# A hybrid decoder trunk on one NeuronCore: outputs of the state-space scan by 64-column blocks

## The chip, the core and the metric

The kernel runs on one core of one Trainium2 chip, in float32. The metric is the device time of the whole program in microseconds. The kernel before takes 884.48 us (median of 3 runs, 884.39 to 885.38).

## The reference, cut to what matters

One sequence of 256 steps and 2048 channels goes through an even layer, an odd layer (differential attention) and a final RMSNorm. The even layer projects to 5120 columns; 1024 of them, `xa`, feed 64 groups of 16 channels, each with 64 complex states. Per group, with A = diag(a) from `lam` and `dt`:

```
h[t] = a * h[t-1] + B u[t]          # complex, 64 states
y[t] = Re(C h[t]) + D u[t]
```

`y` goes through gelu and a gate (`w_glu`), and then, beside a second branch, into the output projection. The inputs are scaled so that all parts count.

## The kernel before, in words

All weights stream from HBM by SP's queue into three buffers `wr` (`fetch`, L144). Each chunk is split into a high and a low part: ACT copies it to `wh`, VectorE subtracts to `wl` (`split`, L169, both at high priority), and TensorE multiplies three times (hi x hi, hi x lo, lo x hi). The layer's projections come in the order v, xa, u, gb, ga, then half of the output projection ("eo"), then "glu" (L802), which needs the state-space output, then the rest. Smaller jobs are generators that are run one step at a time between the chunks (`run_side`, L202).

The order of the instructions on TensorE, VectorE, ACT and POOL is laid by the planner of the tile framework, which simulates the program with costs of its own and takes what is ready by priority: program order, and for blocks in `hp()` a head start of 4000 places. A tile waits for the last use of the tile that had its slot (`t8(slot, ...)`; the pool `t4` has three slots). Only SP's order is by hand. In the trace a float32 matmul that is not float32r leaves two records.

The state-space part works on pairs of steps. `ssm_params` (L388) computes `ab` (a, complex), `fc` and `fa` (the input factors for the second and the first step of a pair) on 128 x 32 tiles. `ssm_consts` (L492) fills `bbr[0..1]`, `cA` and `cN` with zeros on POOL and then makes them by products on VectorE (two of m1, two of m2, then one combination each) and masked copies on ACT (`masked`, L487, two per result): `bbr` = B times fc and fa, `cA` = C times a, `cN` = C. Its last step makes `pk0` with 64 matmuls of 32 weight columns and 32 streamed columns (L533 to L535) and adds it on VectorE into `intra` (L536 to L539): the part K0 = Re(C fc B) of an output that comes from inputs of the same pair at the same step, beside D. The part for the other step of the pair comes with the state.

`ssm_set` (L588) is run eight times, for two halves of the groups, two `qh` and two `q`: W = B u by 16 matmuls (L597), a rotation on VectorE (f), a scan (L613), a rotation back (b), and the state `hst` (L620 to L622) for 128 pairs with a zero ahead, 129 columns. Then the outputs: where q = 0, four matmuls with `intra` (L627); then, for each of four column tiles, four matmuls with 32 weight columns and 128 streamed columns (L635): the first step of a pair takes `cA` on the state ahead of the pair (columns 0 to 127), the second takes `cN` on the state of the pair itself (columns 1 to 128). They write the rows q*64 and q*64 + 32 on of `y`. ACT's gelu (`yaf`) ends a pair of sets.

Slots: `xk` (the input by rows) uses b9 and b10 before `cA` and `cN`; `xsq`, the scratch of the first norm's squares, uses b12 before `U2`, which holds the inputs `u` (ACT copies, L712).

Of the kernel before, what the change touches and what calls it, by code (L numbers as in the profile page):

```python
# [10 lines left out]
F32 = mybir.dt.float32  # L11
# [3 lines left out]
ALU = mybir.AluOpType  # L15
# [14 lines left out]
def hybrid_trunk_kernel(ctx: ExitStack, tc: tile.TileContext, xT, xtok, w_in0, w_glu, w_out0,  # L30
                        w_in1, w_out1, pk, bc, lng, wsp, rope, subln, fnorm, out):
    nc = tc.nc
    V, A, PE, G, SP = nc.vector, nc.scalar, nc.tensor, nc.gpsimd, nc.sync
# [6 lines left out]
    sm = ctx.enter_context(tc.tile_pool(name="sm", bufs=1))  # L40
# [7 lines left out]
    def t8(slot, name, shape, dt=F32):  # L48
        return big.tile(shape, dt, name=name, tag=f"b{slot}")
# [13 lines left out]
    def mul(o, a, b):  # L63
        tt(o, a, b, ALU.mult)

    def add(o, a, b):
        tt(o, a, b, ALU.add)

    def sub(o, a, b):
        tt(o, a, b, ALU.subtract)  # L70
# [7 lines left out]
    def stt(o, a, s, b, op0, op1):  # L78
        V.scalar_tensor_tensor(out=o, in0=a, scalar=s, in1=b, op0=op0, op1=op1)
# [272 lines left out]
    def p32(name, w=32, dt=F32, bufs=1):  # L352
        return sm.tile([128, w], dt, name=name, tag=f"p{w}{name}", bufs=bufs)
# [32 lines left out]
    cst = {}  # L386

    def ssm_params():  # L388
        dt_ = p32("dt")
        exact_exp(dt_, log_dt)  # L390
        yield
        mag = p32("mag")
        z = tr32("lrdt")
        mul(z, lam_re, dt_)
        exact_exp(mag, z)
        r2 = p32("r2")
        mul(r2, mag, mag)
        cst["r2"] = r2
        yield
        ph = tr32("ph")  # L400
        mul(ph, lam_im, dt_)
        k = tr32("ph_k")
        ts(k, ph, 1.0 / (2 * math.pi), ALU.mult)
        ts(k, k, MAGIC, ALU.add)
        ts(k, k, MAGIC, ALU.subtract)
        stt(ph, k, -6.28125, ph, ALU.mult, ALU.add)
        stt(ph, k, -1.93500518798828125e-3, ph, ALU.mult, ALU.add)
        stt(ph, k, -(2 * math.pi - 6.28125 - 1.93500518798828125e-3), ph, ALU.mult, ALU.add)
        y = tr32("ph_y")
        ts(y, ph, 0.5, ALU.mult)  # L410
        z = tr32("ph_z")
        mul(z, y, y)
        s = tr32("ph_s")
        f = math.factorial
        ts(s, z, 1.0 / f(13), ALU.mult)
        for c in (-1.0 / f(11), 1.0 / f(9), -1.0 / f(7), 1.0 / f(5), -1.0 / f(3)):
            stt(s, s, c, z, ALU.add, ALU.mult)
        stt(s, s, 1.0, y, ALU.add, ALU.mult)
        c_ = tr32("ph_c")
        ts(c_, z, -1.0 / f(14), ALU.mult)  # L420
        for c in (1.0 / f(12), -1.0 / f(10), 1.0 / f(8), -1.0 / f(6), 1.0 / f(4), -0.5):
            stt(c_, c_, c, z, ALU.add, ALU.mult)
        ts(c_, c_, 1.0, ALU.add)
        ep = p32("ep", 64).rearrange("p (c m) -> p c m", c=2)
        mul(ep[:, 0, :], s, s)
        ts(ep[:, 0, :], ep[:, 0, :], -2.0, ALU.mult, 1.0, ALU.add)
        stt(ep[:, 1, :], s, 2.0, c_, ALU.mult, ALU.mult)
        yield
        ab = p32("ab", 64).rearrange("p (c m) -> p c m", c=2)
        mul(ab, ep, mag.unsqueeze(1).to_broadcast([128, 2, 32]))  # L430
        den = tr32("den")
        t1 = tr32("t1")
        mul(den, lam_re, lam_re)
        mul(t1, lam_im, lam_im)
        add(den, den, t1)
        V.reciprocal(out=den, in_=den)
        nr = tr32("nr")
        ts(nr, ab[:, 0, :], 1.0, ALU.subtract)
        fc = p32("fc", 64).rearrange("p (c m) -> p c m", c=2)
        t2_ = tr32("t2")  # L440
        mul(t1, nr, lam_re)
        mul(t2_, ab[:, 1, :], lam_im)
        add(t1, t1, t2_)
        mul(fc[:, 0, :], t1, den)
        mul(t1, ab[:, 1, :], lam_re)
        mul(t2_, nr, lam_im)
        sub(t1, t1, t2_)
        mul(fc[:, 1, :], t1, den)
        fa = p32("fa", 64).rearrange("p (c m) -> p c m", c=2)
        mul(t1, fc[:, 0, :], ab[:, 0, :])  # L450
        mul(t2_, fc[:, 1, :], ab[:, 1, :])
        sub(fa[:, 0, :], t1, t2_)
        mul(t1, fc[:, 0, :], ab[:, 1, :])
        mul(t2_, fc[:, 1, :], ab[:, 0, :])
        add(fa[:, 1, :], t1, t2_)
        cst.update(ab=ab, fc=fc, fa=fa, ep=ep)
        yield

        pw = []
        prev = ep  # L460
        for j in range(7):
            sq = tr32("pw_sq", (128, 64)).rearrange("p (c m) -> p c m", c=2)
            m = tr32("pw_m")
            mul(sq, prev, prev)
            add(m, sq[:, 0, :], sq[:, 1, :])
            ts(m, m, -1.0, ALU.mult, 2.0, ALU.add)
            e = p32(f"pw{j}", 64).rearrange("p (c m) -> p c m", c=2)
            sub(e[:, 0, :], sq[:, 0, :], sq[:, 1, :])
            stt(e[:, 1, :], prev[:, 0, :], 2.0, prev[:, 1, :], ALU.mult, ALU.mult)
            mul(e, e, m.unsqueeze(1).to_broadcast([128, 2, 32]))  # L470
            pw.append(e)
            prev = e
        cst["pw"] = pw
        yield

    bbr = [None, None]
# [15 lines left out]
    def ssm_consts():  # L492
        for c in range(2):
            bbr[c] = t8(7 + c, f"bbr{c}", [128, 32, 2, 32])
            G.memset(bbr[c], 0.0)
        cA = t8(9, "cA", [128, 2, 32, 32])
        cN = t8(10, "cN", [128, 2, 32, 32])
        G.memset(cA, 0.0)
        G.memset(cN, 0.0)
        cst.update(cA=cA, cN=cN)  # L500
        b_re, b_im, c_re, c_im = (bct[:, i] for i in range(4))
        for gg in range(2):
            r = slice(gg * 64, gg * 64 + 64)
            h = slice(gg * 16, gg * 16 + 16)
            act(cN[r, 0, :, h], c_re[r], AF.Copy)
            act(cN[r, 1, :, h], c_im[r], AF.Copy, scale=-1.0)
        yield
        for key, z_re, z_im, o_re, o_im, sign in (
                ("fc", b_re, b_im, bbr[0][:, :, 1, :], bbr[1][:, :, 1, :], 1.0),
                ("fa", b_re, b_im, bbr[0][:, :, 0, :], bbr[1][:, :, 0, :], 1.0),  # L510
                ("ab", c_re, c_im, cA[:, 0], cA[:, 1], -1.0)):
            s = cst[key]
            m1 = t4(f"m1{key}", [128, 2, 32, 16])
            m2 = t4(f"m2{key}", [128, 2, 32, 16])
            mul(m1[:, 0], z_re, sc16(s[:, 0, :]))
            mul(m1[:, 1], z_im, sc16(s[:, 1, :]))
            mul(m2[:, 0], z_im, sc16(s[:, 0, :]))
            mul(m2[:, 1], z_re, sc16(s[:, 1, :]))
            sub(m1[:, 0], m1[:, 0], m1[:, 1])
            if sign > 0:  # L520
                add(m2[:, 0], m2[:, 0], m2[:, 1])
            else:
                stt(m2[:, 0], m2[:, 0], -1.0, m2[:, 1], ALU.mult, ALU.subtract)
            masked(o_re, m1[:, 0])
            masked(o_im, m2[:, 0])
            yield

        intra = cst["intra"]
        pk0 = side1("pk0", [128, 16, 32])
        for i in range(16):  # L530
            for q in range(2):
                P = i * 2 + q
                o = pk0[q * 64:q * 64 + 32, i, :]  # L533
                PE.matmul(o, bbr[0][:, P, 1, :], cN[:, 0, P, :], start=True, stop=False)
                PE.matmul(o, bbr[1][:, P, 1, :], cN[:, 1, P, :], start=False, stop=True)  # L535
        for q in range(2):  # L536
            r = slice(q * 64, q * 64 + 32)
            o = intra[r, :, q * 64:q * 64 + 32]
            add(o, pk0[r], o)  # L539
        yield  # L540

    def ssm_bT():
# [39 lines left out]
        yield  # L582

    ya = {}
    hst = sm.tile([128, 2, 4, 129], F32, name="hst", tag="hst")
    G.memset(hst[:, :, :, 0:1], 0.0)

    def ssm_set(S):  # L588
        half, q4 = S // 4, S % 4
        qh, q = q4 // 2, q4 % 2  # L590
# [9 lines left out]
        m1 = t4(f"f1{S}", [128, 2, 4, 128])  # L600
        m2 = t4(f"f2{S}", [128, 2, 4, 128])
# [8 lines left out]
        for c in range(2):  # L610
            for ct in range(4):
                P = (half * 2 + qh) * 8 + ct * 2 + q
# [3 lines left out]
        m1 = t4(f"b1{S}", [128, 2, 4, 128])  # L616
        m2 = t4(f"b2{S}", [128, 2, 4, 128])
        mul(m1, g, erb)
        mul(m2, g, eib)
        h = hst  # L620
        sub(h[:, 0, :, 1:129], m1[:, 0], m2[:, 1])
        add(h[:, 1, :, 1:129], m1[:, 1], m2[:, 0])  # L622
        yield
        if q == 0:
            ya["y"] = side1(f"y{S}", [128, 4, 128], 1)
# [3 lines left out]
        y = ya["y"]  # L629
        for ct in range(4):  # L630
            P = (half * 2 + qh) * 8 + ct * 2 + q
            for i, cm in ((0, cst["cA"]), (1, cst["cN"])):
                o = y[q * 64 + i * 32:q * 64 + i * 32 + 32, ct, :]
                for c in range(2):
                    PE.matmul(o, cm[:, c, P, :], h[:, c, ct, i:i + 128], start=False, stop=c == 1,  # L635
                              skip_group_check=True)
        yield
        if q == 1:
            if "f" not in ya:
# [523 lines left out]
```

## Time and profile before

| what | value |
|---|---|
| runs | 884.39, 884.48, 885.38 us |
| the profiled execution | 885.88 us, its span 884.2 us |
| granted TensorE clock in it | 0.998 of full |
| TensorE (PE) busy | 867.1 us, 98% |
| TensorE weight loads (PEld) busy | 748.3 us, 85% |
| VectorE (DVE) busy | 678.4 us, 77% |
| ScalarE (ACT) busy | 457.5 us, 52% |
| GpSimd (POOL) busy | 36.5 us, 4% |

Times are in microseconds from the start of the span unless marked ns. Engines are named as in the table; SP is the engine whose queue issues most transfers. `128*32 128x128` behind a matmul gives its weights (rows and columns) and what is streamed. A row of the timeline has the start, the time to the end of the last of the x instructions merged in it, the engine, the line and the operation with output and inputs, and in brackets the engine's idle time before it with what ended it. Ends of matmuls are modelled and run over the next start. An idle time in brackets of a matmul is what is left after that.

### The profile page before, as it was taken

What the parts mean: (1) busy time and instruction counts of PE and PEld (TensorE: products, weight loads), DVE (VectorE), ACT (ScalarE), POOL (GpSimd) and SP (SyncE); (2) the same over time, 40 slices, a digit from 0 to 9 for tenths busy, and PEclk for the clock granted to TensorE, in tenths of its full rate; (3) what the DMA queues carried; (4) which work ended last, traced back from release to release, by engine and by line L of the source; (5) the groups of instructions that cost most, each with busy time, mean ns of one, the idle gap of its engine ahead of it and who ended that gap; (6) DMA issues with size and microseconds to landing.
All of it is one profiled execution on the core that took longest, in us unless ns stands there. A gap on an engine that the chain in (4) does not pass through costs nothing.

```text
span 884.2 us, 13006 instructions
## 1 busy us (share of the span) xinstructions
PE 867.1 (98%) x5038; PEld 748.3 (85%) x5038; DVE 678.4 (77%) x1248; ACT 457.5 (52%) x637; POOL 36.5 (4%) x54
## 2 busy tenths in 40 slices
PE   9999999999999999999999999999999999999996
PEld 7799978788999789888788888888888888888885
DVE  8999869999988766577876688667867687665773
ACT  6664862455434655565445544455546544564551
POOL 7100000000000100000000000000000000000001
PEclk9999999999999999999999999999999999999999
DMA  8965452235524655555554555445554555555442
GB/s 289 406 236 193 144 191 95 97 103 184 191 99 145 254 178 184 190 191 171 169 203 153 181 191 191 184 153 184 183 192 154 190 182 189 189 194 199 157 178 95
DMA packets 55166, 160.18 MB, mean 181 GB/s; under 512 B 3392, under 2 KB 37440, under 8 KB 41024
## 3 DMA queue, kind: packets, MB, share of 16 engines
q1 hardware_dynamic: 54240, 155.68, 50.1%
q0 software_dynamic: 576, 3.15, 0.9%
q8 instruction: 39, 0.64, 0.3%
q10 hardware_dynamic: 288, 0.52, 0.2%
q14 instruction: 23, 0.19, 0.1%
HBM read 157.24 MB, written 2.10 MB: 180 GB/s over the span
## 4 chain that ended last, share of the span: by engine, by line
PE 87%; DVE 8%; ACT 2%; issue 1%; DMA 1%; DVEq 0%; ACTq 0%
PE k L251 7%; PE q L251 7%; PE v L225 4%; PE v L226 4%; PE v L224 4%; PE k L252 3%; PE q L252 3%; PE g L226 3%; PE g L225 3%; PE g L224 3%; PE od L225 2%; PE od L224 2%; PE od L226 2%; DVE wl L61 2%; PE ga L237 2%; PE ga L240 2%
## 5 line engine op out<-in xcount | busy, mean ns | idle before, releaser
L82 ACT ACTIVATE wh<-wr 128x1024 fp32r<-128x1024 f32 (+1 forms) x276 | 288.7, 1047 | 339.2 <-PE v L226 59.5
L61 DVE TENSOR_TENSOR wl<-wr,wh 128x1024 fp32r<-128x1024 f32 (+1 forms) x276 | 332.3, 1206 | 135.3 <-ACT wh L82 133.8
L251 PE MATMUL k<-h2p,wh 128*128 128x512 f32 x256 | 90.9, 398 | 1.7 <-DVE rm L61 1.7
L251 PE MATMUL q<-h2p,wh 128*128 128x512 f32 x256 | 90.2, 396 | 0.0
L252 PE MATMUL q<-h2p,wl 128*128 128x256 f32 x256 | 71.9, 284 | 0.2 <-DVE wl L61 0.2
L252 PE MATMUL k<-h2p,wl 128*128 128x256 f32 x256 | 72.0, 282 | 0.0
L251 PEld LDWEIGHTS k<-h2p,wh 128*128 128x128 f32 x256 | 48.1, 188 | 13.3 <-DVE rm L61 2.0
L251 PEld LDWEIGHTS q<-h2p,wh 128*128 128x128 f32 x256 | 47.8, 188 | 10.5
L225 PE MATMUL v<-wl,h2p 128*128 128x512 f32 x128 | 50.8, 397 | 0.0
L225 PE MATMUL g<-wl,h2p 128*128 128x512 f32 x128 | 50.3, 393 | 0.0
L226 PE MATMUL g<-wh,h2p 128*128 128x512 f32 x128 | 50.1, 391 | 0.0
L226 PE MATMUL v<-wh,h2p 128*128 128x512 f32 x128 | 50.0, 391 | 0.0
L224 PE MATMUL g<-wh,h2p 128*128 128x512 f32 x128 | 50.0, 390 | 0.0
L224 PE MATMUL v<-wh,h2p 128*128 128x512 f32 x128 | 50.0, 390 | 0.0
L252 PEld LDWEIGHTS q<-h2p,wl 128*128 128x128 f32 x256 | 48.4, 189 | 1.0 <-DVE wl L61 0.6
L252 PEld LDWEIGHTS k<-h2p,wl 128*128 128x128 f32 x256 | 48.4, 189 | 0.1
L225 PE MATMUL od<-wl,oh 128*128 128x512 f32 x96 | 37.6, 392 | 0.0
L224 PE MATMUL od<-wh,oh 128*128 128x512 f32 x96 | 37.5, 391 | 0.0
L226 PE MATMUL od<-wh,ol 128*128 128x512 f32 x96 | 37.3, 390 | 0.0
L237 PE MATMUL ga<-hh,wh 128*128 128x256 f32 x128 | 36.6, 286 | 0.0
L240 PE MATMUL ga<-hh,wl 128*128 128x256 f32 x128 | 36.5, 287 | 0.0
L239 PE MATMUL ga<-hl,wh 128*128 128x256 f32 x128 | 36.5, 285 | 0.0
(330 smaller groups left out, 2041.1 us busy)
## 6 DMA issues: line engine op xcount, KB each, us to landing
wr<-in_w_in_dram SPq DMA_DIRECT2D x68, 1024.0 KB, 4.8
wr<-in_w_in_dram SPq DMA_DIRECT2D x68, 512.0 KB, 5.2
wr<-in_w_out_dram SPq DMA_DIRECT2D x32, 1024.0 KB, 4.8
wr<-in_w_glu_dram SPq DMA_DIRECT2D x4, 1024.0 KB, 4.7
wr<-in_w_in_dram SPq DMA_DIRECT2D x8, 256.0 KB, 4.9
xk<-in_xtok_dram SPq DMA_DIRECT2D x2, 1024.0 KB, 10.8
xr<-in_xtok_dram POOLq DMA_DIRECT2D x2, 1024.0 KB, 7.2
xt<-in_xT_dram SPq DMA_DIRECT2D x8, 128.0 KB, 4.6
```

What stands on the lines that cost most here:

```text
L61: (eng or V).tensor_tensor(out=o, in0=a, in1=b, op=op)
L82: A.activation(out=o, in_=i, func=f, **kw)
L224: PE.matmul(ps[:, t, :], hi[:, s], wh, start=first and a == 0, stop=False)
L225: PE.matmul(ps[:, t, :], hi[:, s], wl, start=False, stop=False)
L226: PE.matmul(ps[:, t, :], lo[:, s], wh, start=False, stop=last and a == len(ktiles) - 1)
L237: PE.matmul(ps[:, c, :], wh[:, s], hi, start=first and a == 0 and c % 2 == 0, stop=False, skip_group_check=True)
L239: PE.matmul(ps[:, c, :], wh[:, s], lo, start=False, stop=False, skip_group_check=True)
L240: PE.matmul(ps[:, c, :], wl[:, s], hi, start=False, stop=fin, skip_group_check=True)
L251: PE.matmul(ps[:, c, :], wh[:, s], hl, start=first and a == 0, stop=False, skip_group_check=True)
L252: PE.matmul(ps[:, c, T:], wl[:, s], hl[:, 0], start=False, stop=a == len(ktiles) - 1 and not first, skip_group_check=True)
```

## The change: the diff

Both steps of a pair now take their state part from the state ahead of the pair: the weights `cc[c]` hold 64 columns per group pair, C a and C a^2 side by side, and the 16 matmuls of a set become 8 with 64 weight columns. What the second step gets from the inputs of its own pair now lies wholly in `intra`: `pk0` is made with `bbr`'s two halves side by side (64 columns), which gives K0 and K1, the part that goes from the first step's input to the second step's output, in the same matmuls, and two more sums put them in place. `a2` = a^2 is computed for it. `cN` stays for `pk0` and moves to slot b12.

```diff
@@ ssm_params
+        a2 = p32("a2", 64).rearrange("p (c m) -> p c m", c=2)
+        mul(t1, ab[:, 0, :], ab[:, 0, :])
+        mul(t2_, ab[:, 1, :], ab[:, 1, :])
+        sub(a2[:, 0, :], t1, t2_)
+        stt(a2[:, 1, :], ab[:, 0, :], 2.0, ab[:, 1, :], ALU.mult, ALU.mult)
-        cst.update(ab=ab, fc=fc, fa=fa, ep=ep)
+        cst.update(ab=ab, a2=a2, fc=fc, fa=fa, ep=ep)
@@ ssm_consts
-        cA = t8(9, "cA", [128, 2, 32, 32])
-        cN = t8(10, "cN", [128, 2, 32, 32])
-        G.memset(cA, 0.0)
-        G.memset(cN, 0.0)
-        cst.update(cA=cA, cN=cN)
+        cc = [t8(9 + c, f"cc{c}", [128, 32, 2, 32]) for c in range(2)]
+        cN = t8(12, "cN", [128, 2, 32, 32])
+        for z in (cc[0], cc[1], cN):
+            G.memset(z, 0.0)
+        cst["cc"] = cc
...
-                ("ab", c_re, c_im, cA[:, 0], cA[:, 1], -1.0)):
+                ("ab", c_re, c_im, cc[0][:, :, 0, :], cc[1][:, :, 0, :], -1.0),
+                ("a2", c_re, c_im, cc[0][:, :, 1, :], cc[1][:, :, 1, :], -1.0)):
...
-                o = pk0[q * 64:q * 64 + 32, i, :]
-                PE.matmul(o, bbr[0][:, P, 1, :], cN[:, 0, P, :], start=True, stop=False)
-                PE.matmul(o, bbr[1][:, P, 1, :], cN[:, 1, P, :], start=False, stop=True)
+                o = pk0[q * 64:q * 64 + 64, i, :]
+                for c in range(2):
+                    PE.matmul(o, bbr[c][:, P].rearrange("p j h -> p (j h)"), cN[:, c, P, :], start=c == 0, stop=c == 1)
         for q in range(2):
-            r = slice(q * 64, q * 64 + 32)
-            o = intra[r, :, q * 64:q * 64 + 32]
+            r = slice(q * 64, q * 64 + 64)
+            o = intra[r, :, q * 64 + 32:q * 64 + 64]
             add(o, pk0[r], o)
+            o = intra[q * 64:q * 64 + 32, :, q * 64:q * 64 + 32]
+            add(o, pk0[q * 64 + 32:q * 64 + 64], o)
@@ ssm_set
-    hst = sm.tile([128, 2, 4, 129], F32, name="hst", tag="hst")
+    hst = sm.tile([128, 2, 4, 128], F32, name="hst", tag="hst")
...
-        sub(h[:, 0, :, 1:129], m1[:, 0], m2[:, 1])
-        add(h[:, 1, :, 1:129], m1[:, 1], m2[:, 0])
+        sub(h[:, 0, :, 1:128], m1[:, 0, :, 0:127], m2[:, 1, :, 0:127])
+        add(h[:, 1, :, 1:128], m1[:, 1, :, 0:127], m2[:, 0, :, 0:127])
...
-            for i, cm in ((0, cst["cA"]), (1, cst["cN"])):
-                o = y[q * 64 + i * 32:q * 64 + i * 32 + 32, ct, :]
-                for c in range(2):
-                    PE.matmul(o, cm[:, c, P, :], h[:, c, ct, i:i + 128], start=False, stop=c == 1,
-                              skip_group_check=True)
+            for c in range(2):
+                PE.matmul(y[q * 64:q * 64 + 64, ct, :], cst["cc"][c][:, P].rearrange("p i h -> p (i h)"),
+                          h[:, c, ct, :], start=False, stop=c == 1, skip_group_check=True)
```

## Rows read from the trace of the kernel before

**Rows 1.** The page, part 4: the chain that ended last, by engine.
```profile
PE 87%; DVE 8%; ACT 2%; issue 1%; DMA 1%; DVEq 0%; ACTq 0%
```

**Rows 2.** Timeline of TensorE, 150 to 154 us: one set's output matmuls.
```profile
150.33 0.30 PE L635 MATMUL y<-hst,cA 128*32 128x128 f32 x1
150.35 0.30 PE L635 MATMUL y<-hst,cN 128*32 128x128 f32 x1
...
152.03 0.27 PE L635 MATMUL y<-hst,cN 128*32 128x128 f32 x1
```

**Rows 3.** Chain that ended last, in order of time: start, us, what, records.
```profile
177.85 0.34 PE y L635 x2
...
179.97 1.87 PE y L635 x30
...
195.53 1.98 PE W L597 x16
...
303.64 1.90 PE y L635 x32
```

**Rows 4.** Windows: stretch, length, busy of PE, PEld, DVE, ACT, POOL; clock; DMA.
```profile
40.00:60.00 20.00, 19.14 (x109) 16.58 (x108) 19.77 (x104) 12.98 (x21) 1.26 (x1) 1.00 0.75 288
...
80.00:100.00 20.00, 20.00 (x276) 19.65 (x274) 19.50 (x29) 12.43 (x17) 0.00 (x0) 1.00 0.55 202
100.00:120.00 20.00, 19.23 (x100) 15.79 (x98) 15.99 (x31) 17.94 (x23) 0.00 (x0) 1.00 0.30 106
120.00:140.00 20.00, 18.78 (x102) 15.24 (x101) 12.78 (x21) 9.65 (x15) 0.00 (x0) 1.00 0.45 158
...
160.00:180.00 20.00, 18.59 (x118) 14.72 (x119) 19.05 (x29) 7.87 (x10) 0.00 (x0) 1.00 0.34 110
```

**Rows 5.** Timeline of TensorE, 335 to 336 us: the first glu matmul.
```profile
335.30 0.28 PE L237 MATMUL glu<-yah,wh 128*128 128x256 f32 x1
```

**Rows 6.** Lines L535 and L597: weight loads, ns min/median/max, first and last start.
```profile
L535 PEld LDWEIGHTS pk<-cN,bbr x64: 105/113/114, 97.4 to 99.4; 128*32 128x32 f32 x64
...
L597 PEld LDWEIGHTS W<-U,bT x128: 182/188/189, 125.3 to 277.0; 64*128 64x128 f32 x128
```

**Rows 7.** Timelines of POOL, VectorE and TensorE, 34 to 44 us.
```profile
34.38 1.81 POOL L498 MEMSET cA<- 128x2048 f32 x1 [16.31 <-ACT xsq L82]
37.23 1.81 POOL L499 MEMSET cN<- 128x2048 f32 x1 [1.03 <-ACT xsq L82]
...
35.05 1.18 DVE L74 TENSOR_SCALAR ph_c<-ph_c 128x32 f32<-128x32 f32 x1
...
38.50 0.57 DVE L76 TENSOR_SCALAR pw_m<-pw_m 128x32 f32<-128x32 f32 x1
...
39.45 0.16 DVE L76 TENSOR_SCALAR rq_v<-ss 128x2 f32<-128x2 f32 x1
...
43.02 0.50 PE L225 MATMUL v<-wl,hh 128*128 128x512 f32 x1 [0.86 <-DVE wl L61]
43.35 0.39 PE L226 MATMUL v<-wh,hl 128*128 128x512 f32 x1
```

**Rows 8.** Timeline of VectorE, 95 to 113 us.
```profile
95.15 1.28 DVE L61 TENSOR_TENSOR m1ab<-bct,ab 128x512 f32<-128x512 f32 x2
...
99.96 1.38 DVE L61 TENSOR_TENSOR intra<-pk,intra 32x512 f32<-32x512 f32 x2
...
102.09 1.23 DVE L61 TENSOR_TENSOR xs<-xa,rbc 128x1024 f32<-128x1024 f32 x1
...
112.15 1.23 DVE L61 TENSOR_TENSOR wl<-wr,wh 128x1024 fp32r<-128x1024 f32 x1 [3.44 <-ACT wh L82]
```

**Rows 9.** Timelines of ACT and TensorE, 104 to 114 us.
```profile
104.47 1.25 ACT L82 ACTIVATE cA<-m2ab 64x512 f32<-64x512 f32 x2
105.73 5.30 ACT L82 ACTIVATE U<-xs 32x512 f32<-32x512 f32 x8
...
113.43 0.50 PE L225 MATMUL u<-wl,hh 128*128 128x512 f32 x1 [0.77 <-DVE wl L61]
```

## The prediction

> **What bounds the kernel now.** I read the page first, its chain that ended last [rows 1]: TensorE holds 87% of it, VectorE 8%. So time taken from TensorE counts, and a wait added there is paid unless a later wait absorbs it.
>
> Then the timeline of the stretch that the change touches, the state-space outputs "y" [rows 2]. A float32 matmul leaves two records, so the 16 matmuls of a set are 32. The reader should look at the starts, not at the durations: a cA record and a cN record start 20 ns apart, and the sixteenth cN record comes 1.68 us after the first, 15 steps of 112 ns. The two 32-column halves already run beside each other. The chain view gives whole sets [rows 3]: 1.90 us for a set in one block; 0.34 + 1.87 us for one whose first matmul (two records) is issued alone. In the timeline three of the eight sets are of the first kind, five of the second: 3 x 1.90 + 5 x 2.21 = 16.75 us.
>
> Last, busy time by stretches of 20 us, for TensorE's idle time [rows 4]: 0.86 us in 40 to 60, none in 80 to 100, 0.77, 1.22 and 1.41 us in the three rows after; the stretches not shown up to 340 are full or nearly so. The state-space part has slack at its end: the last set ends at 305.5 [rows 3], glu, its user, starts at 335.30 [rows 5], with "eo" matmuls between.
>
> **y matmuls: 128 become 64, no gain.** A set becomes 16 records of 64 columns, one after the other on one half of the columns, with nothing beside them. The stream per record stays at 128 columns. No row shows 64 columns. One end is the pair's pace, 112 ns; the other is W's, the same stream under 128 columns: 1.98 us for 16 records [rows 3], 124 ns. A block has 1.90 - 16 x 0.112 = 0.11 us of entry and exit, the rest of a split set 1.87 - 15 x 0.112 = 0.19. At 112 ns the block stays at 1.90 and the split rest becomes 14 x 0.112 + 0.19 = 1.76: 5 x -0.11 = -0.6 us. At 124 ns: block 2.09, rest 1.93, 3 x 0.19 + 5 x 0.06 = +0.9 us. 64 lies between 32 and 128, so I take the middle, **+0.2 us**. Had the halves been serial, the change would save 128 x 0.112 = 14 us; the starts exclude that.
>
> **pk0: the same 64 matmuls, twice the columns in each.** All but two of its 128 records start between 97.4 and 99.4 [rows 6]: 2.0 us over 125 steps, 16 ns. They go to two column groups (q = 0 and 1) that overlap, so a group spends 32 ns on a record, against a stream of 32/128 x 112 = 28 ns. A weight load takes 113 ns for 32 columns and 188 ns for 128 [rows 6]: 75 ns over 96 columns, 0.78 a column, 25 ns for 32 and 50 for 64. The stream stays, and the load becomes the longer. Lower end: the loads hide, 0. Upper end: loads of the two groups can't go beside each other, 128 x 57 = 7.3, +5.2 us. I take what keeps the groups' overlap that the rows show: 32 + 25 = 57 ns, 64 x 57 = 3.7 us, **+1.7 us**. "xa" matmuls run without a pause on both sides (TensorE is full from 80 to 100 [rows 4]), so it lies on the path.
>
> **A third memset on POOL.** cN now has a fill of its own, 1.81 us like the two of before [rows 7]. Its slot is that of the scratch xsq, which ACT frees when it frees the slot of the second fill (POOL's idle time before 37.23 ends with xsq), so POOL should run it right behind, 39.05 to 40.86. POOL's own time is free. But the VectorE TENSOR_SCALAR issued at 35.05 takes 1.18 us and ends 0.04 us after the first fill, and that of 38.50 takes 0.57 us and ends 0.03 us after the second; the one at 39.45, with no fill beside it, takes 0.16 [rows 7]. It would be held until 40.86, +1.4 us. VectorE's queue is packed (19.77 of 20 us in 40 to 60 [rows 4]), and its weight split is what TensorE waits for at 43.02 [rows 7]; that wait is all the idle time of 40 to 60, so up to 100 nothing gives the delay back. **+1.4 us**. Ends: 0, if VectorE holds no such work then or POOL comes later, and +1.8, a whole fill.
>
> The Trainium skill, SBUF — State Buffer, section "Who interferes with whom", says that whichever of the two engines issues first keeps the shared port for its whole instruction and that the other blocks. The rows agree for a fill that came first; no row shows the other order, in which POOL would wait and this term would be near 0.
>
> **VectorE's and ACT's additions.** VectorE: four a2 products on 32 elements (0.1 us each), seven operations on 512 like "ab" at 1.28/2, and two more intra sums, 1.38 a pair [rows 8]: 0.4 + 4.5 + 1.4 = 6.3 us. ACT: four masked copies at 1.25/2, 2.5 us [rows 9]. The user of the a2 products is the first y at 150.33; before that VectorE idles 3.44 us up to 112.15 [rows 8] and 7.2 us in 120 to 140, ACT over 10 us there [rows 4]. They fit in those holes, and if a hole fails, the state-space chain is later by at most 6.3 us out of 30 us of slack. So **0**. Lower end 0, as work is only added. Upper end: ACT takes the four copies ahead of the eight U copies, behind which the wait at 113.43 stands [rows 9]: +2.5 us. The intra sums stand ahead of xs at 102.09, which would end at 102.09 + 1.4 + 1.23 = 104.7; U starts at 105.73, behind the cA copies, so that is hidden. U now also waits for pk0 (cN's slot), about 101.3, hidden likewise. The state tile loses one column of 129: nothing. No DMA is added or moved, so SP's queue keeps its order.
>
> **Sum.** 0.2 + 1.7 + 1.4 + 0 = +3.3 us. The profiled execution took 885.88 us, 1.7 more than its span and 1.4 more than the median 884.48. The terms are differences: the profiled time of the change would be 889.2, its median **887.8 us**. A difference of 0.2%, 1.8 us, is about the least that a measurement of this kernel can tell from none.
>
> **Rivals.**
> A. The ACT copies go ahead of U: 2.5 more, 890.3. For it: ACT served the cA copies before U at 104.47 [rows 9]. Against: U and the splits have high priority, and the a2 products come last on VectorE.
> B. Both new costs hide: pk0's loads behind its streams, and POOL blocks nobody. 884.5 + 0.2 = 884.7. For it: W hides a load of 188 ns [rows 6]. Against: pk0's stream is a quarter of W's.
> C. Faster. The order on each engine comes from a planner that simulates the program; with 64 matmuls fewer it lays the queues anew, and TensorE's waits between 40 and 180 vanish. The price is the idle time in [rows 4], 4.3 us in five waits, and some 0.17 us more at each, by which a matmul's modelled end runs over the next start (the one at 43.02 lasts 0.50 us, the next starts after 0.33 [rows 7]): 5.1 us, 882.7. It decides the sign only if all of them go, or fewer together with the low ends above. Against: nothing in the change aims at those waits.
> D. The loads of a lone column group show: each y record costs 50 ns more, 128 x 0.050 = 6.4 us, with 3.1 for the other two 894.0. Against: W with its longer loads keeps 124 ns [rows 3, 6], so they hide. The Trainium skill, TensorE: Matmul & The Clock Gate, section "The mechanism", says that a load overlaps running matmuls only where it goes to other rows of the array; by that rule D would hold, as all records of a set use all rows. The trace disagrees: W's records of a set share their rows, and their loads are hidden.
>
> **How the numbers follow.** The forecast's case, with its terms between +1.2 and +6, 0.56 (0.49 above 1.8 us); A 0.12; B 0.18; C 0.11, 0.10 of it faster by over 0.2%; D 0.03. Slower by over 0.2%: 0.49 + 0.12 + 0.03 = 0.64; faster 0.10; within 0.26. The range leaves out C's faster part, D and the top of the forecast's case: from 1.0 below the median, 883.5 (B with y at its low end), to A with 0.7 more, 891.0.
>
> **What would show it.** y: 16 records of 64 columns a set, starts 112 to 124 ns apart, a block of 1.9 to 2.1 us; starts 55 ns apart, or sets of 1 us, would show me wrong. pk0: a block of about 3.7 us. POOL: a third fill from 39 us, a VectorE TENSOR_SCALAR that ends with it, and TensorE's wait at 43 grown from 0.86 to about 2.3 us. ACT: the copies for a2 behind U, and the wait at 113 unchanged. The sum falls if TensorE's idle time drops by over 2 us, or if the planner puts the sets elsewhere among u, gb and ga.

## The result, and the profile after

The changed kernel takes 890.88 us (median of four runs, 889.75 to 892.21) against 884.93 for the kernel before beside it: 1.0063 times as long, 95% interval 1.0051 to 1.0076. Run again with the second group of experiments it was 1.0058 (1.0046 to 1.0071). The forecast was 887.8 us, +3.3; +4.7 to +6 came. The profiled execution took 889.75 us (span 888.0), 3.9 us more than that of before, and is the short one of the four.

By the page, the chain that ended last is now 90% PE and 6% VectorE, where it was 87 and 8 [rows 1]: TensorE still sets the end. What matters lies before "glu", by TensorE's timeline of the changed kernel:

```profile
339.19 0.28 PE L237 MATMUL glu<-yah,wh 128*128 128x256 f32 x1
```

glu starts 3.89 us later than in [rows 5]; behind it the two traces run alike. TensorE's time up to there by tile, each matmul counted up to the start of the next:

| tile | before, us | after, us | difference |
|---|---|---|---|
| v (and psw before it) | 52.76 | 53.35 | +0.59 |
| xa | 46.43 | 49.57 | +3.14 |
| pk (pk0) | 2.33 | 4.09 | +1.76 |
| pbt | 4.75 | 5.07 | +0.32 |
| u | 46.26 | 47.97 | +1.71 |
| y with the states (cA, cN; then cc) | 16.73 | 15.70 | -1.03 |
| y with intra | 5.34 | 3.80 | -1.54 |
| s | 4.38 | 3.49 | -0.89 |
| W, gb, ybT, ga, eo, rbcp | 155.19 | 155.03 | -0.16 |

y and pk0, which the change names, give -1.03 and +1.76. The rest, and most of the loss, is waiting. The stretch where it arises, in windows (stretch, length, busy of PE, PEld, DVE, ACT, POOL; clock; DMA):

```profile
40.00:60.00 20.00, 18.30 (x104) 15.78 (x103) 19.59 (x112) 12.73 (x21) 1.44 (x2) 1.00 0.74 273
100.00:105.00 5.00, 5.00 (x123) 4.69 (x121) 5.00 (x8) 3.16 (x6) 0.00 (x0) 1.00 0.24 70
105.00:110.00 5.00, 2.38 (x34) 1.77 (x30) 4.02 (x8) 4.66 (x8) 0.00 (x0) 0.81 0.34 143
110.00:115.00 5.00, 4.14 (x11) 3.26 (x11) 4.55 (x19) 4.87 (x9) 0.00 (x0) 0.51 0.02 3
115.00:120.00 5.00, 5.00 (x24) 4.09 (x23) 2.51 (x4) 4.96 (x6) 0.00 (x0) 1.00 0.00 0
120.00:140.00 20.00, 19.26 (x100) 15.36 (x99) 10.80 (x10) 10.25 (x14) 0.00 (x0) 1.00 0.46 158
160.00:180.00 20.00, 20.00 (x113) 16.73 (x114) 19.85 (x33) 8.95 (x11) 0.00 (x0) 1.00 0.41 152
```

Against [rows 4]: TensorE is idle for 1.70 us in 40 to 60 (0.86 before) and for 3.5 us in 105 to 115. There the granted clock falls to 0.81 and 0.51, 0.5 being the lower of its two levels. In 120 to 140 and 160 to 180 it loses less than before. Why it stands still at 106, first on TensorE's timeline, then on VectorE's (start, time to the end of the last of x, what, idle time before with its releaser):

```profile
100.17 0.30 PE L544 MATMUL pk<-cN,bbr 128*64 128x32 f32 x2
...
101.94 3.92 PE L544 MATMUL pk<-cN,bbr 128*64 128x32 f32 x126
105.79 0.39 PE L239 MATMUL xa<-hl,wh 128*128 128x256 f32 x1
106.02 0.28 PE L240 MATMUL xa<-hh,wl 128*128 128x256 f32 x1
108.91 1.09 PE L561 MATMUL pbt<-ident,bbr 128*128 128x128 f32 x4 [2.62 <-DVE intra L61]
110.86 0.79 PE L224 MATMUL u<-wh,hh 128*128 128x512 f32 x1 [0.86 <-DVE xs L61]
111.45 0.63 PE L225 MATMUL u<-wl,hh 128*128 128x512 f32 x1
...
115.13 0.40 PE L225 MATMUL u<-wl,hh 128*128 128x512 f32 x1
```

```profile
100.26 1.29 DVE L61 TENSOR_TENSOR m1a<-bct,a 128x512 f32<-128x512 f32 x2
101.46 1.22 DVE L61 TENSOR_TENSOR wl<-wr,wh 128x1024 fp32r<-128x1024 f32 x1
102.60 0.69 DVE L79 SCALAR_TENSOR_TENSOR m2ab<-m2ab 128x512 f32<-128x512 f32 x1
103.20 0.69 DVE L61 TENSOR_TENSOR m1a<-m1a 128x512 f32<-128x512 f32 x1
103.80 1.29 DVE L61 TENSOR_TENSOR m2a<-bct,a 128x512 f32<-128x512 f32 x2
105.97 2.80 DVE L61 TENSOR_TENSOR intra<-pk,intra 64x512 f32<-64x512 f32 x4 [0.88 <-PE pk L544]
108.80 0.69 DVE L79 SCALAR_TENSOR_TENSOR m2a<-m2a 128x512 f32<-128x512 f32 x1
109.41 0.15 DVE L76 TENSOR_SCALAR rq_v<-vss 128x1 f32<-128x1 f32 x1
109.58 1.23 DVE L61 TENSOR_TENSOR xs<-xa,rbc 128x1024 f32<-128x1024 f32 x1
```

xs evacuates xa and frees its PSUM for u. It started at 102.09 [rows 8] and now starts at 109.58, behind the a2 products (m1a, m2a) and behind the four intra sums. These wait for pk0, whose block ends only at 105.79, since it now needs the fa half of bbr too (before, it started at 97.4 [rows 6]). After the stand, eight u matmuls start 0.43 us apart instead of 0.23, until about 114.9.

### The profile page after: what moved, and what is told of

It is laid out like the page before. It is cut to its first block, busy times and chain, and to the rows that moved or that the text cites. A ratio compares the mean times of both kernels' runs of the same rounds, so it can differ in the third digit from the quotient of the medians.

```text
span 888.0 us, 12770 instructions
## 1 busy us (share of the span) xinstructions
PE 868.6 (98%) x4910; PEld 749.4 (84%) x4910; DVE 683.8 (77%) x1260; ACT 463.0 (52%) x643; POOL 39.6 (4%) x55
## 4 chain that ended last, share of the span: by engine, by line
PE 90%; DVE 6%; ACT 1%; DMA 1%; issue 1%; DVEq 0%; ACTq 0%
PE k L251 7%; PE q L251 7%; PE v L225 3%; PE k L252 3%; PE v L226 3%; PE v L224 3%; PE q L252 3%; PE g L226 3%; PE g L225 3%; PE g L224 3%; PE od L225 2%; PE od L224 2%; PE od L226 2%; DVE wl L61 2%; PE W L608 2%; PE y L644 2%
## 5 line engine op out<-in xcount | busy, mean ns | idle before, releaser
L240 PE MATMUL xa<-hh,wl 128*128 128x256 f32 x128 | 36.2, 284 | 0.1
```

What stands on the lines that cost most here:

```text
L240: PE.matmul(ps[:, c, :], wl[:, s], hi, start=False, stop=fin, skip_group_check=True)
```

## The theories

T: the loss is pk0's wider records (+1.75), the third fill on POOL, and VectorE's order ahead of xs, which makes TensorE idle and then lets it run at the lower clock; y and some later waits give a part back. Rivals: R1, the 64-column y records cost; R2, pk0's later place alone makes pbt and u late; and, told for each run, that a delay is taken up by another wait. Each ratio below is against the kernel before, run beside it.

## Experiment 1: one part at a time

**e1: pk0 alone.** Kernel before, with

```diff
-                o = pk0[q * 64:q * 64 + 32, i, :]
-                PE.matmul(o, bbr[0][:, P, 1, :], cN[:, 0, P, :], start=True, stop=False)
...
+                o = pk0[q * 64:q * 64 + 64, i, :]
+                for c in range(2):
+                    PE.matmul(o, bbr[c][:, P].rearrange("p j h -> p (j h)"), cN[:, c, P, :], start=c == 0, stop=c == 1)
...
```

> The kernel before with pk0 alone changed: 64 columns a record (K0 and K1 are both made, K0 alone is summed, by two sums); y, the fills and the products stay as before. In the instruction order xs stands ahead of the intra sums. Theory T (the wider block itself costs 1.75 us; the rest of the loss comes from xs standing behind the a2 products and the sums on VectorE): pk0's records at 31 ns, a block of 3.85 us, xs near 102, no TensorE idle time over 1.5 us between 105 and 112, granted clock 1.0 there; 884.9 + 1.8 = 886.7, 886 to 887.5. Rival R2 (pk0's later place by itself, as it now needs the fa half of bbr, makes pbt and u late): the idle time of about 4.5 us and the low clock at 108 to 115 show here too, 889 to 890.5.

Measured: 884.52 us, 0.9989 (0.9980 to 0.9997), a little under the kernel before. pk0 is as wide and as late as in the changed kernel, and yet xs is early. Of e1's timelines, TensorE's and VectorE's:

```profile
100.61 3.93 PE L535 MATMUL pk<-cN,bbr 128*64 128x32 f32 x126
```

```profile
101.36 1.22 DVE L61 TENSOR_TENSOR xs<-xa,rbc 128x1024 f32<-128x1024 f32 x1 [0.52 <-ACT vscr L82]
```

By these rows of TensorE's and VectorE's timelines R2 falls: lateness alone stops nothing. But T's time was 2 us too high, as two waits of before, pbt at 131 and gb at 173 (the idle time of 160 to 180 in [rows 4]), were gone. TensorE's timeline of before:

```profile
131.57 0.65 PE L550 MATMUL pbt<-ident,bbr 128*128 128x128 f32 x4 [0.76 <-ACT bT L82]
...
173.25 0.50 PE L224 MATMUL gb<-wh,hh 128*128 128x512 f32 x1 [1.41 <-ACT ut L82]
```

**e2: y without pk0's part.** Changed kernel, with pk0 and its sums as before:

```diff
-                o = pk0[q * 64:q * 64 + 64, i, :]
+                o = pk0[q * 64:q * 64 + 32, i, :]
...
-                    PE.matmul(o, bbr[c][:, P].rearrange("p j h -> p (j h)"), cN[:, c, P, :], start=c == 0, stop=c == 1)
+                    PE.matmul(o, bbr[c][:, P, 1, :], cN[:, c, P, :], start=c == 0, stop=c == 1)
...
```

> The changed kernel with pk0 as before (32 columns, K0 alone, two sums of K0); y by 64 columns, the a2 products and the third fill stay. Left out: what the second step of a pair gets from the inputs of its own pair. In the instruction order the a2 products still stand ahead of xs, the sums no longer wait for a late pk0. Theory T: y -1.0, fill +0.6, no wider block, xs behind the a2 products (about 4 us later than before), so some TensorE idle time at 106 to 112 (2 to 4 us) and perhaps a stretch of low clock, less later waits: 886 to 888. Rival R2 (the late pk0 alone is the cause): xs early enough, no idle time, 884.9 - 1.0 + 0.6 = 884.5, 884 to 885. Rival R1 (the 64-column y records themselves cost): the y sets take longer than the 16.75 us of before.

Measured: 894.27 us, 1.0092 (1.0079 to 1.0106), longer than the whole change. pk0 is early and narrow here (its block ends at 101.4), yet xs stands at 110.03, behind the a2 products, and u waits for it, by TensorE's timeline of e2:

```profile
111.31 0.79 PE L224 MATMUL u<-wh,hh 128*128 128x512 f32 x1 [5.49 <-DVE rq_i L76]
```

The window 110 to 115 has clock 0.53, and u waits 2.08 us more at 123.75 for a weight split. The direction is T's, the size is not: I had 2 to 4 us of idle time and perhaps a low clock. R1 falls: the y records take 15.99 us here, under the 16.73 of before.

**e5: the fill alone.** Kernel before, with

```diff
         G.memset(cN, 0.0)
+        G.memset(cN, 0.0)
```

> The kernel before with the fill of cN issued twice, nothing else; VectorE's order of before stays. Theory T (a third fill on POOL holds VectorE up, and TensorE pays for it at its wait near 43): the VectorE operation that starts behind the second fill ends with the third, near 40.9, the wait of 0.86 us becomes 1.7 to 2.2, +0.6 to +1.4 us: 885.5 to 886.3. Rival (POOL's third fill blocks nobody, or the delay is absorbed up to 100): 884.9, within 0.2 us of before.

Measured: 886.59 us, 1.0011 (1.0002 to 1.0020), +1.0 by the medians. The third fill runs from 37.70 to 39.52, and VectorE stops with it. VectorE's and TensorE's timelines of e5:

```profile
38.05 1.48 DVE L76 TENSOR_SCALAR rq_v<-ss 128x2 f32<-128x2 f32 x1
...
38.46 1.11 DVE L566 COPY E<-pw 128x32 f32<-128x32 f32 x1
39.57 0.17 DVE L76 TENSOR_SCALAR rq_i<-rq_v 128x2 int32<-128x2 int32 x1
```

```profile
42.65 0.50 PE L225 MATMUL v<-wl,hh 128*128 128x512 f32 x1 [1.61 <-DVE wl L61]
```

TensorE's wait of 0.86 [rows 7] is 1.61, so the fill alone adds 0.75 us to it. The price on the whole program rests on the medians, +1.0 us with an interval of 0.2 to 1.8: in the profiled execution, the shortest of the eleven, the first v matmuls ran 1.1 us earlier than in the trace of before, and glu starts at 334.93 against 335.30.

**e11: the a2 products late.** Changed kernel; the products for a2 are cut out of the loop of `ssm_consts` into a generator and run behind xs:

```diff
+        if half == 0:
+            for _ in cst["a2_job"]():
+                pass
         for _ in ssm_half(half):
             pass
```

> The whole change, but the a2 products (VectorE and ACT) are issued behind xs of the first half, so that in the instruction order xs stands ahead of them and of the four intra sums. Theory T (VectorE's queue ahead of xs is the larger part of the loss): xs at about 102 to 103.5, TensorE idle time at 106 to 112 under 2 us, clock 1.0 there; the block of pk0 (+1.75), the fill (+0.6) and y (-1.0) stay: 884.9 + 1.4 = 886.3, and as low as 884.5 if the waits of 112 to 180 that vanished in the changed kernel stay away. Rival (the place of xs is not the cause; pk0's late place and its lane in PSUM are): still over 3 us of idle time at 106 to 112, and 889.5 to 891.

Measured: 889.69 us, 1.0041 (1.0029 to 1.0054). The place is T's, the time the rival's. xs is at 103.66, and the stand and the low clock are gone, by the windows of e11:

```profile
105.00:110.00 5.00, 5.00 (x77) 4.47 (x74) 4.96 (x9) 4.16 (x7) 0.00 (x0) 1.00 0.33 134
110.00:115.00 5.00, 4.04 (x20) 2.92 (x19) 3.39 (x11) 4.91 (x8) 0.00 (x0) 1.00 0.00 0
```

But the waits of 131 and 173 are back (0.76 at 135.63, 1.41 at 177.35), and the fill cost more: a VectorE operation was held through two fills, and TensorE's wait was 2.23 us. In the profiled execution, the shortest of the five, glu starts 2.7 us later than in [rows 5]; the rest of the 4.1 us by the medians is not accounted for. VectorE's timeline of e11:

```profile
38.50 2.23 DVE L76 TENSOR_SCALAR pw_m<-pw_m 128x32 f32<-128x32 f32 x1
```

## Experiment 2: the two losses crossed

**f1: the changed kernel again.** No edit.

> The changed kernel itself, beside the three variants that follow, on the same chip. All theories: 889.5 to 892.5, TensorE idle for 3 to 5 us and at a low granted clock between 105 and 115.

Measured: 890.51 us, 1.0058 (1.0046 to 1.0071). Here 12 u matmuls started 0.43 us apart, against eight in the profile above: the length of the stretch at the lower clock differs from run to run.

**f2: the fill on ACT.** Changed kernel, with

```diff
-        for z in (cc[0], cc[1], cN):
+        for z in (cc[0], cc[1]):
             G.memset(z, 0.0)
...
+        act(cN.rearrange("p c m h -> p (c m h)").rearrange("p (a b) -> p a b", b=128),
+            ident.unsqueeze(1).to_broadcast([128, 16, 128]), AF.Copy, scale=0.0)
```

> The changed kernel with the fill of cN on ACT in place of POOL; the order of VectorE around xs stays that of the changed kernel (a2 products, four intra sums, then xs). Theory T (two separate losses: the third fill on POOL, 0.8 to 1.7 us, and xs behind the a2 products): the wait at 43 is back at about 0.9 us, the idle time and the low clock at 105 to 115 stay: 1.0 to 1.7 us under the changed kernel beside it, some 889 to 890. Rival (ACT has no room for the fill, so that weight copies come late): a new wait on wh before 80, no gain.

Measured: 889.03 us, 1.0039 (1.0026 to 1.0052), 1.5 us under f1. The wait at 43 is 1.46 where f1 has 2.23, so not all of it goes: ACT's fill, or the four small a2 operations on VectorE, keep the rest (it is 1.46 to 1.50 in all four kernels with the fill on ACT: f2, g1, f4, h2). The stand stays, by the windows of f2:

```profile
105.00:110.00 5.00, 1.53 (x11) 1.07 (x9) 4.69 (x8) 4.63 (x8) 0.00 (x0) 0.86 0.20 80
110.00:115.00 5.00, 4.90 (x12) 3.83 (x13) 3.81 (x19) 4.87 (x9) 0.00 (x0) 0.50 0.00 0
```

**e13: the scratch of a2 in another pool.** Changed kernel; for a2, m1 and m2 are made in two halves in the pool t2:

```diff
+            halves_ = 2 if key == "a2" else 1
...
+                m1, m2 = ((t2 if key == "a2" else t4)(f"m{i}{key}{z}", [128, 2, n, 16]) for i in (1, 2))
```

> The changed kernel with the scratch of the a2 products, in two halves, in the pool t2 in place of t4; nothing else. In the instruction order xs then stands ahead of the a2 products and of the intra sums, pk0 stands wholly behind xa, and two W sets stand between u and gb, as in the changed kernel. The fill stays on POOL. Theory T: no idle time over 1.5 us and clock 1.0 between 105 and 115; pk0 +1.75, fill +0.8 to +1.7, y -0.9 and the waits of 131 and 173 gone (-2.2): 885.6 - 0.6 to 885.6 + 0.4, so 885 to 886. Rival (some other part of the change than the place of xs makes TensorE idle): 3 us or more of idle time stay, 888 to 891.

Measured: 892.35 us, 1.0088 (1.0074 to 1.0102): a miss. The planner moved the fc and fa products back as well, the masks that pk0 needs came at 106.2, and pk0 stood behind the whole of xa. TensorE's timeline of e13:

```profile
105.03 0.27 PE L549 MATMUL pk<-cN,bbr 128*64 128x32 f32 x2 [2.28 <-issue]
105.23 0.66 PE L566 MATMUL pbt<-ident,bbr 128*128 128x128 f32 x4
106.28 0.94 PE L549 MATMUL pk<-cN,bbr 128*64 128x32 f32 x25 [0.39 <-ACT bbr L82]
```

xs was at 108.80 all the same. I had read the order of the queue and not asked when its head could run. The profile names no releaser for the 2.28 us; in g1 the same wait, 2.24 us, ends with ACT's copy into bbr. So R2 has a true core: where nothing is left of xa to cover it, the late pk0 does stop TensorE.

**g1: both.** The edits of f2 and e13 together.

> Both together: the fill of cN on ACT and the scratch of the a2 products in t2. Theory T: the two losses are separate and add, so it lies 1.0 to 1.7 us under the kernel with the scratch alone: 885.6 + 1.75 - 0.9 - 2.2 = 884.2, 883.5 to 885, at or a little under the kernel before. Rival (the losses are one and the same, VectorE being late either way): no difference to the kernel with the scratch alone.

Measured: 889.92 us (887.77 to 891.38), 1.0048 (1.0036 to 1.0061). The level is wrong for e13's reason, but the fill has a price here too: 2.4 us less than e13. The spread of 3.6 us goes with the granted clock of the whole run: 0.997 in the shortest, 0.988 in the longest.

## Experiment 3: what the later pk0 is worth, and a way out

**e14: pk0 late, but narrow.** Kernel before; only the first two of pk0's matmuls read the fa half, with an unused upper part:

```diff
...
+                w = 64 if P < 1 else 32
+                o = pk0[q * 64:q * 64 + w, i, :]
+                for c in range(2):
+                    bq = bbr[c][:, P].rearrange("p j h -> p (j h)")[:, 64 - w:]
+                    PE.matmul(o, bq, cN[:, c, P, :], start=c == 0, stop=c == 1)
```

> The kernel before, in which the first two of pk0's 64 matmuls have 64 columns (the upper 32 are not used), so that pk0 waits for the fa half of bbr as in the changed kernel, while the other 62 stay at 32 columns. Theory T, as the run of the 64-column pk0 alone left it (the later place of pk0 lets the instruction order put xs ahead of the intra sums, and the waits of before at 131 and 173 go; the wider records then cost 1.75 us on top): pk's block at 16 to 17 ns a record, no wait over 0.6 us between 100 and 180, about 1.7 us under the run with 64 columns throughout: 882.5 to 883.5, under the kernel before. Rival (the width has no price on the path, or the waits went for another reason): 884 to 886.

Measured: 882.52 us (882.44 to 882.59), 0.9962 (0.9949 to 0.9976): 3.3 us under the kernel before, and under both kernels. The 126 records take 2.37 us (19 ns each; 3.85 us in e1), and of the waits of before from 97 to glu (five) two are left, by the list of TensorE's waits in e14:

```profile
PE u L224 <- ACT ut L82: 0.4, 1, 0.4
PE eo L225 <- DVE wl L61: 0.2, 1, 0.2
```

The width costs 2.0 us between e1 and e14 (1.5 of it in pk0's block), and the new order of the queues that the later pk0 brings gives 3.3. How: the planner puts xs ahead of the intra sums, and later a set of W (one; the expectations counted two) between u and gb, which covers the ACT gelu that gb waited for. TensorE's timeline of e14:

```profile
166.74 2.05 PE L599 MATMUL W<-U,bT 64*128 64x128 f32 x16
...
169.63 0.47 PE L224 MATMUL gb<-wh,hh 128*128 128x512 f32 x1
```

**f4: the whole change, a2 late, fill on ACT.** The edits of e11 and f2 together.

> The whole change, with the a2 products behind xs and the fill of cN on ACT. In the instruction order the sets between u and gb stand as in the kernel before, so the waits at about 135 and 177 should stay. Theory T: the run with the a2 products late was 4.1 above the kernel before; without the POOL fill it loses 1.0 to 1.5 of that: 2.6 to 3.1 above, so 888 to 888.7; clock 1.0 at 105 to 115. Rival (the fill's delay is taken up by a later wait): no gain, 889 to 890.

Measured: 885.73 us, 1.0004 (0.9995 to 1.0013): level with the kernel before, 3.3 under f2, and better than I expected. From e11 it gains 1.3 us in v by the traces, of which 0.65 lies ahead of the fills and so is not theirs, and 0.4 to 0.9 each in xa, pbt and u behind it. The wait for gb stays (TensorE's waits of f4, 97 to 340):

```profile
PE gb L224 <- ACT ut L82: 1.4, 1, 1.4
```

**h2: the a2 products on POOL.** f4, with the six operations of 512 elements for a2 on POOL (G):

```diff
+                eng = G if key == "a2" else V
...
-                mul(m1[:, 0], z_re, sc16(s[:, 0, :]))
+                tt(m1[:, 0], z_re, sc16(s[:, 0, :]), ALU.mult, eng)
```

> The whole change; the fill of cN on ACT, and the six 512-element operations for a2 on POOL behind xs instead of on VectorE. In the instruction order xs stands ahead of the sums and two W sets stand between u and gb. Theory T: pk0 +1.75, y -0.9, no fill on POOL, no idle time and clock 1.0 at 105 to 115, the waits of before at 131 and 173 gone (-2.2): 885.6 - 1.3 = 884.3, 883.5 to 885.5. Rival (POOL's products hold VectorE up, as its fills did): VectorE operations of 1 us and more between 104 and 115 that end with a POOL operation, 885.5 to 888.

Measured: 887.03 us, 1.0015 (1.0006 to 1.0024); the rival. A set of W stands between u and gb and the wait for gb is gone, but POOL holds VectorE up again: small operations that take 0.2 us elsewhere end where a POOL operation ends (104.51, 110.06). VectorE's timeline of h2:

```profile
103.56 0.97 DVE L79 SCALAR_TENSOR_TENSOR rq_z<-rq_i,rq_v 128x1 f32<-128x1 f32 x1
...
108.72 1.36 DVE L79 SCALAR_TENSOR_TENSOR rq_z<-vrs,rq_v 128x1 f32<-128x1 f32 x1
```

ACT now has a pair of a2 copies between two weight copies, and u waits 1.15 us for the weight split behind them (0.77 before [rows 9]): the cost that rival A of the prediction described, though behind U and not ahead of it. ACT's timeline of h2:

```profile
110.48 1.06 ACT L82 ACTIVATE wh<-wr 128x1024 fp32r<-128x1024 f32 x1
111.44 1.25 ACT L82 ACTIVATE cc<-m1a 64x512 f32<-64x512 f32 x2
112.72 1.06 ACT L82 ACTIVATE wh<-wr 128x1024 fp32r<-128x1024 f32 x1
```

## Why the prediction was right, and where it was not

**The sign** was right, and pk0 and the fill did cost. But most of the loss came from a third term that I had set to 0, less what rival C described. That 890.88 lies within the range is luck: the range ends at 891.0 because of rival A, which cost nothing here, and the loss that filled it had no place in the sum.

**y, +0.2: -1.03.** The halves did run beside each other, as the starts of [rows 2] said, and 64 columns keep that pace. The chain that ended last in the changed kernel, in order of time:

```profile
158.02 1.89 PE y L644 x16
...
260.82 1.67 PE y L644 x14
```

A block stays at 1.89. The rest of a split set has 14 records and takes 1.67: two records fewer save 0.22, or 0.11 each, and in the trace the starts behind the first step lie 109 ns apart. I had put 1.76. That, and four splits instead of five, is the gain. My upper end was misread: 1.98 us for W's 16 records, 124 ns each, counts entry and exit, while in the trace of before the starts of W's records lie 112 ns apart behind the first step. So both ends had the same pace, and the term should have been -0.6. Rival D's rule would have made each record some 50 ns longer; the loads of 64 columns (137 ns each) are hidden. So the Trainium skill's rule (TensorE: Matmul & The Clock Gate, "The mechanism"), that loads overlap only on other rows, is not what this trace shows.

**pk0, +1.7: +1.76.** 31 ns a record, where I had 57 for two. e14 shows 1.5 us of it the other way round. That the longer load sets this pace was argued from [rows 6] and not tested by itself.

**The third fill, +1.4: at the wait at 43, +0.84 in the profile, +0.75 in e5, +1.4 in e11 and f1.** The mechanism held. (The table has only +0.59 for v, as the matmuls ahead of the fills ran 0.25 us earlier in that execution. From f1 to f2 the medians fall by 1.5: 0.8 at this wait, 0.7 in xa's row.) The operation caught is the one I had named. It was held for 1.60 us, but in this execution the stretch began 0.5 us earlier (first fill at 33.85, 34.38 in [rows 7]), and TensorE's wait at 43 rose by 0.84 only. In e11 and f1 another was caught, and the wait is 2.23, the 1.4 more that I had taken. POOL's and VectorE's timelines of the changed kernel:

```profile
36.69 1.81 POOL L506 MEMSET cc<- 128x2048 f32 x1 [1.03 <-ACT xsq L82]
38.44 1.84 POOL L506 MEMSET cN<- 128x2048 f32 x1
```

```profile
38.71 1.60 DVE L76 TENSOR_SCALAR rq_v<-ss 128x2 f32<-128x2 f32 x1
...
40.34 0.17 DVE L76 TENSOR_SCALAR rq_i<-rq_v 128x2 int32<-128x2 int32 x1
```

**"VectorE's and ACT's additions ... So 0": the step that failed.** Two sentences of it. "The user of the a2 products is the first y at 150.33" looked at who needs the a2 products and not at who stands behind them: the planner takes what is ready, so they ran ahead of xs and pushed it back by their own time. "The intra sums stand ahead of xs at 102.09, which would end at 102.09 + 1.4 + 1.23 = 104.7" used pk0's old time; pk0 had come to need the fa half, so four sums waited at 105.97. Together xs is 7.5 us later, against the 2.4 us that I had allowed before U. TensorE lost 2.8 us from the end of xa to pbt, 1.5 around pbt and, at the lower clock, 2.0 in u: 6.3 us. f2 and f4 differ in the place of the a2 products alone and put their net price at 3.3 us with the fill on ACT; f1 and e11, with the fill on POOL, put it at 0.6. Two slips changed nothing: six operations on 512 elements are added, not seven, and B with y at its low end is 883.9, not 883.5.

**Rival C, 0.11, slower in the sum but real.** The waits at 131 and 173 did go in the changed kernel (120 to 140 and 160 to 180 in the windows above). The one at 173 is most of the -1.54 of the table; the one at 131 lies in pbt's row, where the stand's 1.5 covers it; another, of 0.46 at 135, is most of the -0.89 of s. I had given it a chance only as a whole and no share in the sum. In e14 re-laid queues alone, from another cause than the one I had named, give 3.3 us, more than half of the 5.1 priced for it.

**Rival A**: its order came, its cost did not. ACT made both pairs of a2 copies ahead of U (104.61 and 109.52), where I had expected them behind it, but U, at 110.84, had to wait for xs, which ended at 110.81, in any case.

The sum that the runs leave: f4, with the fill on ACT and the a2 products late, is level with the kernel before (up to glu pk0 +1.76, y -0.88, and 1.6 less in pbt, u, ga and others, by its trace). So the two together carry the whole 4.7 us of the changed kernel beside them (f1). How it splits between them depends on the order: over the kernel before, f1 has 4.7, f2 3.2, e11 4.1 and f4 nothing (medians, each with an interval of about 1 us either way), so the fill on ACT gains 1.5 with the a2 products early and 4.2 with them late, and the late products gain 0.6 with the fill on POOL and 3.3 with it on ACT. The two are not separate, as T had it: 2.7 us went only when both were mended, and the runs don't show why.

Open: why the planner lays a set of W between u and gb in some kernels and not in others; of the versions of the whole change, only h2 has both xs early and that set, and there POOL's products cost time. A higher place for xs by itself was not tried. For f2's wait of 1.46 at 43, ACT's fill and the small a2 operations were not told apart.

## What to carry to other kernels

When work is added to an engine with holes in it, look first at what it will stand ahead of, not at where it could fit: an operation that is ready early runs early, and the one that frees the next stage's PSUM pays. Where an operand of an old step grows, take the time at which its newest part is ready and move every user of that step with it. And where a scheduler orders the queues, price its re-laying as a term of its own, both ways: here a dependency without any use (e14) was worth 3.3 us, more than pk0's wider records cost.

## What the runs showed of the hardware beyond that

The stand of TensorE near 106 (in e13 and g1 some us earlier, ahead of pk0) cost more than its length. In the six profiles that have it (two of the changed kernel, e2, f2, e13, g1) the granted clock right behind it is 0.50 to 0.56 in one of the rows of 5 us, close to the lower level, while TensorE is at work again: u goes at 0.43 us a matmul for 0.23, pk0 in g1 at 55 ns a record for 31. In the five kernels without the stand (e1, e11, e14, f4, h2) it is 1.00 from 100 to 120. The experiments did not take the clock and the idle time apart.

A single VectorE operation of 128x32 elements was held for 2.23 us through two fills on POOL that followed each other (e11). POOL's products held VectorE's small operations up as well (h2), while the intra sums beside them, one input of which is in PSUM, took 0.70 us each as in the changed kernel. The Trainium skill, SBUF — State Buffer, section "Who interferes with whom", says that a VectorE instruction with two SBUF inputs contends with a GpSimd instruction that reads SBUF; the rows of h2 agree.
